# Weight pairs of the heads scaled on GpSimd, with the half-width low parts made there

## The chip, the cores and the metric

One core of one Trainium2 chip runs the whole program. Its engines are TensorE (PE: products and transposes, with the weight load PEld), VectorE (DVE), ScalarE (ACT) and GpSimd (POOL); each works through its own instructions in order and waits where one of them needs what another engine has not finished. The on-chip memory is SBUF, the product banks are PSUM, and SyncE (SP) issues DMA transfers from and to HBM. The metric is the device time of one execution in microseconds (us), as the median of several.

## The reference, cut to what matters

The layer normalises 2048 tokens of width 1024 (and 256 context tokens), multiplies them by one matrix `w_in` of 9216 columns, and splits the columns between a gated recurrence with eight heads of width 128 (five column blocks a head: query, value, two forget gates, output gate) and a short convolution (four times 1024 columns). Both meet in an output projection:

```python
h = rmsnorm(x, norm_w[l]) * (1.0 + scale[:, None]) + shift[:, None]
hc = rmsnorm(xc, norm_w[l]) * (1.0 + scale_c) + shift_c
p = h @ w_in[l]
pc = hc @ (w_in[l, :, :HG_COLS] if last else w_in[l])
...
o, _, _ = bidir_scan(q, kf, kb, v, gf, gb, s_f, s_b)
y_hg = hgrn_out(o, p[..., 4 * HG_WIDTH:HG_COLS], hg_onorm_w[l], x.dtype)
y_cv = conv_branch(p[..., HG_COLS:], conv_w[l], grid=True)
y = jnp.concatenate([y_hg, y_cv], axis=-1) @ w_out[l]
x = x + gate[:, None] * y
return rmsnorm(x, final_norm_w)
```

What this case turns on is the product `h @ w_in`, in float32.

## The kernel before

**Products in float16 parts.** A float32 operand is scaled by a power of two and kept as a float16 high part and a float16 low part (the rest); a product is then three float16 products (high by high, high by low, low by high: lines 930 to 932). `split` (L155 to L158) makes both parts of a piece of a weight block: ACT writes the high part with the scale as a factor, and DVE's SCALAR_TENSOR_TENSOR multiplies the piece by the scale again and subtracts the high part.

**Seven products for eight.** Columns are taken in pairs of blocks of 128. With the pair as a 2x2 arrangement of half-width operands, `seven` (from L917) forms the four results from seven products, in the order A11, S1, S2, A12, S3, S4, A22. Its banks are `sa`, `sb`, `sc`; `keep` (L937) is ACT's copy of a bank out of PSUM (`p1`, `p5`, `u2`), which the product that goes on in the same bank waits for, and `plus` (L941) is DVE's sum of a bank and such a copy, into `f`, `vT`, `q` or `z`. A unit is one such set of seven products for 512 tokens.

**Preparing a pair.** `load_pair` loads two blocks of the weights, 128x1024 float32 each, into `stage` (in the profile `ws_p`; `ws_p281` is block 1 of pair p28, `ws_p280` its block 0). The steps in `w.pre` have ACT sum the absolute values (L409); the nine steps in `w.rest` are: `begin` (the scale `sc_p` by three small DVE instructions at L151 to L153, and the sum S1, `s1_p`, at L424), `whole` (A11 and A12 at once: high part `whia`, low part `wloa`, 128x1024; then block 1's left half becomes A11 minus A21, L435), S1 (`whib`, `wlob`), `sum_a` (S2, over block 0's left half, L441), A22, S2, `sum_b` (S4, over block 0's right half, L444), S3, S4. The last three land in `e_p`. S1, A22, S2, S3 and S4 are 128x512 each. A pair has 128x1024 and five times 128x512 to split. The sums and differences are made of the unscaled blocks, and the scale comes in at each `split`. The first pair of each kind gets A21 too, in a place of its own (`a21_at`), for products that aren't in the scheme of seven.

There are 36 pairs: eight z pairs (the two forget gates of a head, p24 to p31), eight v pairs (value and query, p8 to p15), four gate pairs (p32 to p38, for two heads each), and sixteen of the convolution. `split_steps` hands out the steps of the next pair while a unit's products run, one each few ticks of PE: in the heads `w.gap` is 6 ticks and `w.room` 4.

**What runs beside it.** The loop goes over 8 heads by 4 segments of 512 tokens; units of the next segment run while the scan of the segment before is computed, from `chain`. A scan has seven levels. `update` (L485 on `K`, L492 on `Q`, L498 on `tot`, all DVE) works them out; ACT makes the copy `km` (L601), POOL the copy `qm` (L608, three in a segment), and PE multiplies them (L631, L650, L657) into `A`, from which DVE takes `Ac` (L639). At the end of the levels ACT copies `A` (L661) and POOL writes four diagonal pieces of `Ac` over it (L665). So before the change POOL has two kinds of work in a segment, three `qm` and four `A`.

**What sets the order.** The program is written step by step, then a scheduler of the language lays each engine's instructions in order by when it reckons them ready; the order on an engine is fixed from then on. So a step that waits longer can be put behind another.

Of the kernel before, what the change touches and what calls it, by code (L numbers as in the profile page):

```python
# [14 lines left out]
AF = mybir.ActivationFunctionType  # L15
ALU = mybir.AluOpType
# [3 lines left out]
P = 128  # L20
# [13 lines left out]
HEADS = 8  # L34
# [26 lines left out]
def hybrid_layer(ctx: ExitStack, tc, x, cx, w_ada, b_ada, w_in, w_out, fnorm_w, small_d, masks, ident_d, sel_d, out):  # L61
    nc = tc.nc
    V, S, G, PE, SY = nc.vector, nc.scalar, nc.gpsimd, nc.tensor, nc.sync
# [76 lines left out]
    def pow2_scale(rs, nm, keep=False, room=0, rb=None):  # L140
        ps = px_t(f"ss_{nm}")
        if rb is None:
            rb = sp.tile([P, 1], BF16, tag="rb", name=f"rb_{nm}", bufs=4)
            V.tensor_copy(rb, rs)
        PE.matmul(ps[:, :1], sub(rb, 0, [[0, P]]), rb, start=True, stop=True)
        if keep:
            st = cp.tile([P, 4], F32, name=f"sc_{nm}")
        else:
            st = sp.tile([P, 4], F32, tag="scale", name=f"sc_{nm}", bufs=12)
        sti = st.bitcast(I32)  # L150
        V.tensor_scalar(sti[:, 2:3], ps[:, :1].bitcast(I32), 24, None, ALU.logical_shift_right)  # L151
        V.tensor_scalar(sti[:, 0:1], sti[:, 2:3], -EXP_UNIT, (204.0 - room) * EXP_UNIT, ALU.mult, ALU.add)
        V.tensor_scalar(sti[:, 1:2], sti[:, 2:3], EXP_UNIT, (50.0 + room) * EXP_UNIT, ALU.mult, ALU.add)  # L153
        return st

    def split(st, src, hi, lo):
        S.activation(hi, src, AF.Copy, scale=st[:, 0:1])  # L157
        V.scalar_tensor_tensor(lo, src, st[:, 0:1], hi, ALU.mult, ALU.subtract)  # L158
# [80 lines left out]
    lows, casts = {}, {}  # L239
# [151 lines left out]
    def behind(fn):  # L391

        follow(last_keep, fn)

    def load_pair(col0, col1, nm, own=False, a21_at=None):

        w = W()
        stage, rs = [], []
        for i, c0 in enumerate((col0, col1)):
            sg_ = wp.tile([P, KT, P], F32, tag="stage", name=f"ws_{nm}{i}", bufs=4)  # L400
            SY.dma_start(sg_, w_in[c0 // P])
            stage.append(sg_)
        a11, a12 = stage[0][:, :HK], stage[0][:, HK:]
        a21, a22 = stage[1][:, :HK], stage[1][:, HK:]
        t = {}

        def sizes(i):
            r = sp.tile([P, 1], F32, tag="rowsum", name=f"rsum_{nm}{i}", bufs=4)
            S.activation(junk.rearrange("p (k n) -> p k n", k=KT), stage[i], AF.Abs, accum_out=r)  # L409
            rs.append(r)  # L410
            if i:
                rs.append(sp.tile([P, 1], BF16, tag="rb", name=f"rb_{nm}", bufs=4))
                S.activation(rs[2], rs[1], AF.Identity, bias=rs[0])

        def begin():
            w.st = pow2_scale(None, nm, rb=rs[2])
            pool, x = (qp, "g") if own else (wp, "w")
            nb = 1 if own else 2
            t["a"] = [pool.tile([P, KT, P], F16, tag=f"{x}{y}", name=f"w{y}a_{nm}", bufs=2 * nb) for y in ("hi", "lo")]
            t["b"] = [pool.tile([P, KT, P], F16, tag=f"{x}{y}", name=f"w{y}b_{nm}", bufs=2 * nb) for y in ("hi", "lo")]  # L420
            ee = pool.tile([P, 2, 3 * HK, P], F16, tag="ge" if own else "e", name=f"e_{nm}", bufs=nb)
            t["e"] = [ee[:, 0], ee[:, 1]]
            t["s1"] = rp.tile([P, HK, P], F32, tag="ring", name=f"s1_{nm}")
            V.tensor_tensor(t["s1"], a21, a22, ALU.add)  # L424
            w.ops = {}
            for i, (key, o) in {"A11": ("a", 0), "A12": ("a", HK), "A22": ("b", 0), "S1": ("b", HK), "S2": ("e", 0),
                                "S3": ("e", HK), "S4": ("e", 2 * HK)}.items():
                w.ops[i] = [x_[:, o:o + HK] for x_ in t[key]]
            if a21_at is not None:
                w.ops["A21"] = a21_at  # L430
                split(w.st, a21, *a21_at)

        def whole():
            split(w.st, stage[0], t["a"][0], t["a"][1])
            V.tensor_tensor(a21, a11, a21, ALU.subtract)  # L435

        def part(name, src):
            return lambda: split(w.st, src(), *w.ops[name])

        def sum_a():  # L440
            V.tensor_tensor(a11, t["s1"], a11, ALU.subtract)  # L441

        def sum_b():
            V.tensor_tensor(a12, a12, a11, ALU.subtract)  # L444

        w.pre = [lambda: behind(lambda: sizes(0)), lambda: behind(lambda: sizes(1))]
        w.rest = [begin, whole, part("S1", lambda: t["s1"]), sum_a, part("A22", lambda: a22),
                  part("S2", lambda: a11), sum_b, part("S3", lambda: a21), part("S4", lambda: a12)]
        block = col0 // P - 5 * HEADS
        w.gap, w.room = (6, 4) if block < 0 else (2, {0: 3, 1: 2}.get(block % 8, 1))  # L450
        return w

# [871 lines left out]
    def load(own):  # L1324
        wk = todo[own].pop(0)
        ws[wk] = load_pair(wk[0], wk[1], f"p{wk[0] // P}", own, extra_a21[own].pop(0) if extra_a21[own] else None)
        loaded.append(ws[wk])
        return ws[wk]
# [356 lines left out]
```

## Time and profile before

| | us |
|---|---|
| median of 3 runs | 2149.01 |
| lowest, highest | 2147.64, 2150.84 |
| profiled execution, span of core 0 | 2150.1 |
| PE busy | 2073.2 |
| DVE busy | 1645.8 |
| ACT busy | 1192.2 |
| POOL busy | 191.8 |

The profile gives a span and no time around it, so the span is what stands beside the runs. A row with a time ahead is an instruction: its start in us from the start of the span, its length in us, the engine, the line of the kernel, the operation, what it writes and reads with the numbers of the buffers left out, the size, and in brackets how long the engine stood idle before it and what ended that. A row that begins with a line number is a group of such instructions, with their number, busy us and mean ns, then the idle time before them.

```profile
PE   5988999999999999999999999999999999999998
PEld 2877878888888888888888887444444444444443
DVE  6787988878778787788687887678778656687775
ACT  7965666757567666576676654354445423333332
POOL 0121111111111110111110100000000000000000
```

These are the engines' busy shares in 40 slices of the span, in tenths. The norms and the conditioning come first, then the heads (to about 1270 us), the convolution and at the end the output projection. POOL has a tenth or two to do in the heads and next to nothing behind them.

### The profile page before, as it was taken

The page shows a single profiled execution, that of the slowest core. Times are in us where ns is not written, and L with a number is a line of the kernel's source. Part 1 is how long each engine was busy: PE and PEld are TensorE (multiplying, and loading weights), DVE is VectorE, ACT ScalarE, POOL GpSimd, SP SyncE. Part 2 cuts the span into 40 slices and gives each one's busy share as a digit, 9 for nine tenths or more (in the row PEclk, how much of TensorE's full clock was granted, in tenths as well). Part 3 has the DMA queues.
Part 4 walks back from the last instruction along what each step waited for, and adds up shares of the span by engine and source line. Part 5 has one row for each costly group of instructions (what it writes and reads, how often), then busy time and mean ns, then how long its engine had stood idle before and what let it go on. Part 6 is the DMA issues. An engine that isn't in the chain of part 4 may idle for free.

```text
span 2150.1 us, 53050 instructions
## 1 busy us (share of the span) xinstructions
PE 2073.2 (96%) x22111; PEld 1466.0 (68%) x22111; DVE 1645.8 (77%) x3413; ACT 1192.2 (55%) x2406; POOL 191.8 (9%) x272
## 2 busy tenths in 40 slices
PE   5988999999999999999999999999999999999998
PEld 2877878888888888888888887444444444444443
DVE  6787988878778787788687887678778656687775
ACT  7965666757567666576676654354445423333332
POOL 0121111111111110111110100000000000000000
PEclk9999999999999999999999999999999999999999
DMA  9567533442344233424543458933442105642421
GB/s 356 191 207 265 178 126 134 137 158 72 114 129 146 97 114 109 153 81 142 194 131 127 130 165 260 285 108 110 134 149 93 54 23 196 206 143 92 137 79 59
DMA packets 185798, 311.02 MB, mean 145 GB/s; under 512 B 13010, under 2 KB 114770, under 8 KB 183764
## 3 DMA queue, kind: packets, MB, share of 16 engines
q1 hardware_dynamic: 183396, 303.68, 42.9%
q8 instruction: 173, 2.83, 0.5%
q10 hardware_dynamic: 2160, 3.93, 0.5%
q14 instruction: 69, 0.57, 0.1%
HBM read 240.19 MB, written 67.37 MB: 143 GB/s over the span
## 4 chain that ended last, share of the span: by engine, by line
PE 65%; DVE 18%; ACT 7%; DMA 4%; issue 3%; POOL 1%; SPq 0%; POOLq 0%; ACTq 0%; DVEq 0%
PE sa L930 8%; PE sa L932 8%; PE sa L931 8%; PE sb L930 4%; PE sb L932 4%; PE sb L931 4%; PE sa_o L930 2%; PE sa_o L931 2%; PE sa_o L932 2%; DVE Q L492 2%; PE sc L930 2%; PE sc L931 2%; PE sc L932 2%; DVE K L485 2%; PE T L681 2%
## 5 line engine op out<-in xcount | busy, mean ns | idle before, releaser
L931 PEld LDWEIGHTS <-e_p 128*128 128x128 f16 x1332 | 130.4, 98 | 59.8 <-issue 10.3
L930 PEld LDWEIGHTS <-e_p 128*128 128x128 f16 x1332 | 130.4, 98 | 54.0 <-issue 1.1
L601 ACT ACTIVATE km<-K 128x512 f32<-128x512 f32 x192 | 129.6, 675 | 67.2 <-DVE K L485 61.1
L932 PEld LDWEIGHTS <-e_p 128*128 128x128 f16 x1332 | 130.3, 98 | 51.4
L485 DVE TENSOR_TENSOR K<-K,tot 128x512 f32<-128x512 f32 x192 | 132.2, 689 | 42.9 <-ACT km L601 25.3
L492 DVE TENSOR_TENSOR Q<-Q,tot 128x512 f32<-128x512 f32 x192 | 132.5, 690 | 34.9 <-POOL qm L608 19.5
L608 POOL COPY qm<-Q 128x512 f32<-128x512 f32 x96 | 80.8, 842 | 794.4 <-DVE Q L492 778.7
L931 PEld LDWEIGHTS <-whib_p 128*128 128x128 f16 x888 | 86.9, 98 | 42.1 <-issue 8.8
L930 PEld LDWEIGHTS <-whib_p 128*128 128x128 f16 x888 | 86.8, 98 | 36.7 <-issue 0.8
L930 PEld LDWEIGHTS <-whia_p 128*128 128x128 f16 x888 | 87.0, 98 | 35.7 <-DMA hop3B<-Hd3B 2.3
L932 PEld LDWEIGHTS <-wloa_p 128*128 128x128 f16 x888 | 87.0, 98 | 34.2
L931 PEld LDWEIGHTS <-whia_p 128*128 128x128 f16 x888 | 87.0, 98 | 33.9 <-issue 1.5
L932 PEld LDWEIGHTS <-wlob_p 128*128 128x128 f16 x888 | 86.8, 98 | 34.0
L157 ACT ACTIVATE e_p<-ws_p,sc_p 128x512 f16<-128x512 f32 x108 | 77.5, 718 | 54.9 <-DVE ws_p L444 42.0
L665 POOL COPY A<-Ac 32x128 f32<-32x128 f32 x128 | 77.2, 603 | 128.3 <-ACT A L661 110.6
L853 ACT ACTIVATE cv<-c,small 128x512 f32<-128x512 f32 (+1 forms) x36 | 24.2, 673 | 106.8 <-DVE c L871 61.1
L937 ACT ACTIVATE u<-sa,sx_w 128x256 f32<-128x256 f32 (+1 forms) x111 | 58.1, 524 | 43.5 <-PE sa L932 34.7
L937 ACT ACTIVATE p<-sa,sx_w 128x256 f32<-128x256 f32 (+1 forms) x111 | 57.4, 517 | 39.9 <-PE sa L932 39.8
L158 DVE SCALAR_TENSOR_TENSOR e_p<-ws_p,sc_p,e_p 128x512 f16<-128x512 f32 x108 | 79.4, 750 | 0.0
L409 ACT ACTIVATE junk<-ws_p 128x1024 f16<-128x1024 f32 x72 | 75.7, 1052 | 6.5 <-DMA ws_p<-in_w_in 6.3
L1596 POOL TENSOR_TENSOR x_o<-x_o,fw 128x512 f32<-128x512 f32 x1 | 1.3, 1262 | 868.0 <-ACT junk L1587 868.0
L937 ACT ACTIVATE p<-sb,sx_w 128x256 f32<-128x256 f32 (+1 forms) x111 | 57.8, 521 | 30.8 <-PE sb L932 28.0
(858 smaller groups left out, 7036.3 us busy)
## 6 DMA issues: line engine op xcount, KB each, us to landing
ws_p<-in_w_in SPq DMA_DIRECT2D x72, 512.0 KB, 4.3
y_o<-yT SPq DMA_DIRECT2D x32, 512.0 KB, 4.3
xt_x<-in_x SPq DMA_DIRECT2D x16, 512.0 KB, 6.2
wa<-in_w_ada SPq DMA_DIRECT2D x16, 512.0 KB, 10.2
Gd<-zs SPq DMA_DIRECT2D x32, 256.0 KB, 2.7
sg<-Gd SPq DMA_DIRECT2D x32, 256.0 KB, 4.4
wos<-in_w_out SPq DMA_DIRECT2D x32, 256.0 KB, 5.0
yT<-y SPq DMA_DIRECT2D x32, 256.0 KB, 2.9
```

The source lines that it names most:

```text
L157: S.activation(hi, src, AF.Copy, scale=st[:, 0:1])
L158: V.scalar_tensor_tensor(lo, src, st[:, 0:1], hi, ALU.mult, ALU.subtract)
L409: S.activation(junk.rearrange("p (k n) -> p k n", k=KT), stage[i], AF.Abs, accum_out=r)
L485: V.tensor_tensor(m, m, sub(cur, nb + 1, [[2, np_], [-(nb + 1), 2], [0, B]]), ALU.mult)
L492: V.tensor_tensor(m, m, sub(cur, 1, [[2, np_], [nb - 1, 2], [0, B]]), ALU.mult)
L601: S.activation(sub(s.km, 0, [[2 * B, n // (2 * B)], [B, 2], [1, B]]), mix(s.K, n, B, n // (2 * B)), AF.Copy)
L608: G.tensor_copy(sub(qm, 0, [[2 * B, n // (2 * B)], [B, 2], [1, B]]), mix(s.qf, n, B, n // (2 * B)))
L665: G.tensor_copy(A3[js, :, js], s.Ac[js])
L930: PE.matmul(ps, hi[:, k], rh, start=start and k == 0, stop=False, skip_group_check=not start)
L931: PE.matmul(ps, hi[:, k], right(name, 1, k), start=False, stop=False, skip_group_check=not start)
L932: PE.matmul(ps, lo[:, k], rh, start=False, stop=k == nk - 1, skip_group_check=not start)
L937: last_keep.append(S.activation(r, ps, AF.Copy, scale=sx))
```

## The change

For a pair of the heads that has no place for A21 (`scaled`), POOL multiplies both staged blocks by the scale in place, ahead of the first sum. Everything behind that works on scaled values: ACT copies the high parts without a factor, the five half-width low parts are a subtraction on POOL, and the low part of A11 and A12 together a subtraction on DVE. The other pairs (the first z, v and gate pair, and the convolution's) go through `split` as before. Multiplying by a power of two is exact, so what is computed stays the same.

```diff
         t = {}
+        block = col0 // P - 5 * HEADS
+        scaled = block < 0 and a21_at is None
...
             t["s1"] = rp.tile([P, HK, P], F32, tag="ring", name=f"s1_{nm}")
+            if scaled:
+                for i in (1, 0):
+                    G.tensor_scalar(stage[i], stage[i], w.st[:, 0:1], 0.0, ALU.mult, ALU.add)
             V.tensor_tensor(t["s1"], a21, a22, ALU.add)
...
+        def lows(src, hi, lo, eng):
+            if not scaled:
+                return split(w.st, src, hi, lo)
+            S.activation(hi, src, AF.Copy)
+            eng.tensor_tensor(lo, src, hi, ALU.subtract)
+
         def whole():
-            split(w.st, stage[0], t["a"][0], t["a"][1])
+            lows(stage[0], *t["a"], V)
             V.tensor_tensor(a21, a11, a21, ALU.subtract)

         def part(name, src):
-            return lambda: split(w.st, src(), *w.ops[name])
+            return lambda: lows(src(), *w.ops[name], G)
```

The lines move by some: S1's sum from L424 to L429, the difference from L435 to L446, `sum_a` from L441 to L452, `sum_b` from L444 to L455, and all behind them by 10 (`Q` from L492 to L502, `keep` from L937 to L947). The scalings are L428, the copies to the high parts L441, the low parts L442.

Three places show what the order becomes. All are around z pair p28, which is prepared for head 4 while segment 1 of head 3 is scanned (`Q_3_1`, `K_3_1`, `A_3_1`); its scale is `sc_p28`. First DVE, before:

```order
L492 TENSOR_TENSOR Q_3_1_9844<-Q_3_1_9844,tot_3_1_9867 128x32x2x8
L424 TENSOR_TENSOR s1_p28_10104<-ws_p281_8003 128x512
L485 TENSOR_TENSOR K_3_1_9341<-K_3_1_9341,tot_3_1_9867 128x16x2x16
L435 TENSOR_TENSOR ws_p281_8003<-ws_p280_8001,ws_p281_8003 128x512
L151 TENSOR_SCALAR sc_p28_10095<-ss_p28_10093 128x1
L152 TENSOR_SCALAR sc_p28_10095<-sc_p28_10095 128x1
L153 TENSOR_SCALAR sc_p28_10095<-sc_p28_10095 128x1
...
L492 TENSOR_TENSOR Q_3_1_9844<-Q_3_1_9844,tot_3_1_9867 128x16x2x16
...
L485 TENSOR_TENSOR K_3_1_9341<-K_3_1_9341,tot_3_1_9867 128x8x2x32
...
L492 TENSOR_TENSOR Q_3_1_9844<-Q_3_1_9844,tot_3_1_9867 128x8x2x32
L158 SCALAR_TENSOR_TENSOR wloa_p28_10100<-ws_p280_8001,sc_p28_10095,whia_p28_10099 128x1024
L158 SCALAR_TENSOR_TENSOR wlob_p28_10102<-s1_p28_10104,sc_p28_10095,whib_p28_10101 128x512
```

And the same place on DVE now:

```order
L502 TENSOR_TENSOR Q_3_1_9858<-Q_3_1_9858,tot_3_1_9881 128x32x2x8
L495 TENSOR_TENSOR K_3_1_9355<-K_3_1_9355,tot_3_1_9881 128x16x2x16
L151 TENSOR_SCALAR sc_p28_10109<-ss_p28_10107 128x1
...
L502 TENSOR_TENSOR Q_3_1_9858<-Q_3_1_9858,tot_3_1_9881 128x16x2x16
L429 TENSOR_TENSOR s1_p28_10118<-ws_p281_8015 128x512
L649 COPY_PREDICATED Ac_3_1_9937<-mask_127,A4_3_1_10122 128x128
L446 TENSOR_TENSOR ws_p281_8015<-ws_p280_8013,ws_p281_8015 128x512
L649 COPY_PREDICATED Ac_3_1_9937<-mask_127,A4_3_1_10122 128x128
L495 TENSOR_TENSOR K_3_1_9355<-K_3_1_9355,tot_3_1_9881 128x8x2x32
L442 TENSOR_TENSOR wloa_p28_10114<-ws_p280_8013,whia_p28_10113 128x1024
L502 TENSOR_TENSOR Q_3_1_9858<-Q_3_1_9858,tot_3_1_9881 128x8x2x32
```

The scale stands ahead of the sum (L429) and the difference (L446), which stood ahead of it; both now wait for POOL, and so do the `K` and `Q` of level 5 that stand behind them on DVE. `wloa` has moved ahead of that `Q`.

Second ACT, beside it, before (`p5_55` and `u2_55` are `keep`'s copies for a unit's products that are running, `km5_3_1` and `km0_3_0` copies for the scan):

```order
L937 ACTIVATE p5_55_10146<-sb_55_10076,sx_w47_8422 128x256
L157 ACTIVATE whia_p28_10099<-ws_p280_8001,sc_p28_10095 128x1024
L937 ACTIVATE u2_55_10169<-sa_55_10038,sx_w47_8422 128x256
L157 ACTIVATE whib_p28_10101<-s1_p28_10104,sc_p28_10095 128x512
L157 ACTIVATE whib_p28_10101<-ws_p281_8003,sc_p28_10095 128x512
L157 ACTIVATE e_p28_10103<-ws_p281_8003,sc_p28_10095 128x512
L601 ACTIVATE km0_3_0_10514<-K_3_0_9815 128x512
```

And now:

```order
L947 ACTIVATE p5_55_10162<-sb_55_10090,sx_w47_8436 128x256
L611 ACTIVATE km0_3_0_10532<-K_3_0_9829 128x512
L441 ACTIVATE whia_p28_10113<-ws_p280_8013 128x1024
L947 ACTIVATE u2_55_10185<-sa_55_10052,sx_w47_8436 128x256
L441 ACTIVATE whib_p28_10115<-s1_p28_10118 128x512
L441 ACTIVATE whib_p28_10115<-ws_p281_8015 128x512
L441 ACTIVATE e_p28_10117<-ws_p281_8015 128x512
```

`km0` has moved ahead of `whia`, and `whia`, which now waits for POOL's second scaling, still stands right ahead of `u2`.

Third POOL. Before, this stretch holds the scan's copies alone:

```order
L608 COPY qm1_3_1_9954<-Q_3_1_9844 128x512
L608 COPY qm3_3_1_10057<-Q_3_1_9844 128x512
L608 COPY qm5_3_1_10186<-Q_3_1_9844 128x512
L665 COPY A_3_1_10245<-Ac_3_1_9923 32x4x32 x4
L608 COPY qm1_3_0_10604<-Q_3_0_10294 128x512
```

And now, with p12, the v pair of head 4, behind p28 (its low parts left out here):

```order
L618 COPY qm3_3_1_10071<-Q_3_1_9858 128x512
L428 TENSOR_SCALAR ws_p281_8015<-ws_p281_8015,sc_p28_10109 128x1024
L428 TENSOR_SCALAR ws_p280_8013<-ws_p280_8013,sc_p28_10109 128x1024
L618 COPY qm5_3_1_10202<-Q_3_1_9858 128x512
L442 TENSOR_TENSOR wlob_p28_10116<-s1_p28_10118,whib_p28_10115 128x512
L442 TENSOR_TENSOR wlob_p28_10116<-ws_p281_8015,whib_p28_10115 128x512
L442 TENSOR_TENSOR e_p28_10117<-ws_p281_8015,e_p28_10117 128x512
L442 TENSOR_TENSOR e_p28_10117<-ws_p280_8013,e_p28_10117 128x512
L675 COPY A_3_1_10261<-Ac_3_1_9937 32x4x32 x4
L442 TENSOR_TENSOR e_p28_10117<-ws_p280_8013,e_p28_10117 128x512
L428 TENSOR_SCALAR ws_p121_10105<-ws_p121_10105,sc_p12_10437 128x1024
L428 TENSOR_SCALAR ws_p120_10103<-ws_p120_10103,sc_p12_10437 128x1024
```

`qm5` stands behind both scalings of p28, the four `A` copies behind four of its low parts, and the `qm1` of the next segment behind everything of p12.

More of the change, by code (lines that the diff above doesn't have):

```diff
@@ L448, in load_pair @@
                   part("S2", lambda: a11), sum_b, part("S3", lambda: a21), part("S4", lambda: a12)]
-        block = col0 // P - 5 * HEADS
         w.gap, w.room = (6, 4) if block < 0 else (2, {0: 3, 1: 2}.get(block % 8, 1))
```

## The prediction

> **What bounds the kernel now.** I read the page's busy times first, then busy times by stretch, then the waits of TensorE (PE), and last the timeline around one weight pair.
>
> ```profile
> span 2150.1 us, 53050 instructions
> ...
> PE 2073.2 (96%) x22111; PEld 1466.0 (68%) x22111; DVE 1645.8 (77%) x3413; ACT 1192.2 (55%) x2406; POOL 191.8 (9%) x272
> ...
> 470.00:610.00 140.00, 138.24 (x2137) 122.63 (x2139) 109.23 (x240) 86.42 (x197) 18.18 (x24) 1.00 0.35 111
> 610.00:760.00 150.00, 147.35 (x2241) 130.35 (x2230) 121.59 (x272) 99.81 (x221) 21.92 (x32) 1.00 0.38 125
> ```
>
> The first two lines are the page's: PE is busy for 96% of the span. The other two are stretches inside the heads; after start, end and length their columns are PE, its weight loads, VectorE (DVE), ScalarE (ACT), GpSimd (POOL), then the granted clock, which is full. In the first stretch PE is busy for 138.24 of 140 us, DVE for 109.23 (78%), ACT for 86.42 (62%), POOL for 18.18 (13%). So work taken from DVE is not taken from the time: at most PE's 1.8 us of idle time in such a stretch can be won, and whatever makes PE wait longer is paid in full.
>
> PE's waits in the heads (190 to 1270 us), the largest; each row names the product that waits, what it waits for, and us in total, times, the longest:
>
> ```profile
> PE A L631 <- POOL qm L608: 7.6, 10, 2.7
> PE sa L930 <- ACT u L937: 3.3, 11, 0.6
> PE sa L930 <- DVE f L941: 3.1, 7, 1.2
> PE A L650 <- POOL qm L608: 2.7, 2, 1.5
> PE A L631 <- DVE Q L492: 2.1, 8, 0.3
> PE T L681 <- ACT kT L674: 1.6, 3, 0.8
> PE sa L930 <- ACT p L937: 1.6, 2, 1.1
> PE sb L930 <- DVE f L941: 1.3, 1, 1.3
> ```
>
> They come to 23.3 us. Many are short, which says that ACT's and DVE's evacuations of the product banks (`u`, `p`, `f`) arrive close to the moment PE needs them. That closeness decides this case.
>
> **The change part by part.** It touches 17 weight pairs: seven z pairs, seven v pairs, three gate pairs (eight, eight and four there are; the first of each kind has a place for A21 and stays as it was). For each:
>
> *DVE loses work.* The five half-width low parts leave it:
>
> ```profile
> L158 DVE SCALAR_TENSOR_TENSOR e_p<-ws_p,sc_p,e_p 128x512 f16<-128x512 f32 x108 | 79.4, 750 | 0.0
> ```
>
> Five of 750 ns are 3.75 us a pair, 64 us in all. The full-width low part stays, as a subtraction without the scale; I cost that difference at nothing. ACT keeps its instructions at their sizes, only without a scale: nothing.
>
> *POOL gains work.* Two scalings of 128x1024 and five subtractions of 128x512 a pair. Nearest rows:
>
> ```profile
> 632.85 0.61 POOL L608 COPY qm<-Q 128x512 f32<-128x512 f32 x1 [3.54 <-DVE Q L492]
> ...
> 2132.68 1.26 POOL L1596 TENSOR_TENSOR x_o<-x_o,fw 128x512 f32<-128x512 f32 x1 [868.04 <-ACT junk L1587]
> ```
>
> A one-input pass over 512 columns takes 0.61 us undisturbed, so 1024 columns are put at 1.22. A two-input pass takes 1.26. That is 2x1.22 + 5x1.26 = 8.7 us a pair, 148 us in all; POOL has the room (18 of 140 us used). The bounds for one subtraction are 0.61 (as if the second input cost nothing) and 1.26 plus one wait for DVE of 0.69, so 1.95; I take 1.26, the row of the same operation.
>
> [...]
>
> *The operands themselves are not late.* The z pair that is prepared at 640 us, in front of head 4's first unit:
>
> ```profile
> 648.00 1.40 DVE L158 SCALAR_TENSOR_TENSOR e_p<-ws_p,sc_p,e_p 128x512 f16<-128x512 f32 x2
> ...
> 659.08 0.27 PE L930 MATMUL sa<-hop15B,whia_p 128*128 128x256 f16 x1
> ...
> 632.90:669.40 36.50, 35.94 (x491) 31.56 (x488) 34.52 (x73) 27.91 (x51) 5.60 (x7) 1.00 0.20 65
> ```
>
> Its last two low parts end at 649.4, and PE reads the pair first at 659.08. POOL needs 8.7 us for what DVE did in about 5, so the last low part comes some 4 to 6 us later and is still in time. What costs is who waits meanwhile, and the third row says that this is a tight place: between 632.9 and 669.4, where a z pair and a v pair are prepared beside a scan, DVE works for 34.52 of 36.5 us and PE for 35.94.
>
> *The new wait in a z pair.* Before:
>
> ```profile
> 637.43 0.14 DVE L153 TENSOR_SCALAR sc_p<-sc_p 128x1 int32<-128x1 int32 x1
> ...
> 637.83 0.69 DVE L492 TENSOR_TENSOR Q<-Q,tot 128x512 f32<-128x512 f32 x1
> ...
> 639.24 1.14 ACT L157 ACTIVATE whia_p<-ws_p,sc_p 128x1024 f16<-128x1024 f32 x1
> 640.27 0.46 ACT L937 ACTIVATE u<-sa,sx_w 128x256 f32<-128x256 f32 x1
> ...
> 640.79 0.27 PE L930 MATMUL sa<-hop15T,e_p 128*128 128x256 f16 x1 [0.27 <-ACT u L937]
> ...
> 642.98 0.63 PE L657 MATMUL A<-Q,K 128*32 128x64 f32 x32
> ```
>
> The scale is ready at 637.57. Behind it POOL now runs two scalings, to 640.0, or to 640.7 if DVE's `Q` (0.69) gets between them. `whia` on ACT waits for the second: it ends at 641.2 to 641.9, and `u`, which stands right behind it on ACT, at 641.6 to 642.3. Before, `u` ended at 640.73 and PE, already waiting, went on at 640.79. So PE stands 0.9 to 1.6 us longer. DVE's queue gives about the same: the sum and the difference wait for the scalings, then come `K`, `wloa`, and `Q` of level 5, which also needs POOL's copy `qm` that is queued behind the scalings; `Q` ends near 643.9 to 644.6, against PE's need at 642.98 plus the stall. The four `A` copies of the level results, which PE's next products need, now stand on POOL between low parts. Lower end: nothing, if the scheduler's new place of `whia` happened to be covered by another wait of PE; the rows show none there. Upper end: 1.6 us, as worked out. I take the upper end, **1.6 us**, because the five POOL subtractions that follow contend with DVE as well.
>
> *The new wait in a v pair.* Before:
>
> ```profile
> 659.00 0.15 DVE L153 TENSOR_SCALAR sc_p<-sc_p 128x1 int32<-128x1 int32 x1
> ...
> 659.12 1.15 ACT L157 ACTIVATE whia_p<-ws_p,sc_p 128x1024 f16<-128x1024 f32 x1 [2.71 <-DVE sc_p L152]
> 660.17 0.58 ACT L740 ACTIVATE Q<-o 128x512 f32<-128x512 f32 x1
> ...
> 666.98 0.49 ACT L937 ACTIVATE u<-sa,sx_w 128x256 f32<-128x256 f32 x1
> ...
> 667.51 0.27 PE L930 MATMUL sa<-hop15T,e_p 128*128 128x256 f16 x1
> ```
>
> The scale comes earlier, near 657.8, since the sum and the difference (about 0.69 each) now stand behind it; two scalings end at 660.3 to 661.0, so `whia` begins 1.2 to 1.9 us later. Copy `Q` (0.58) goes ahead of it and gives 0.5 back. ACT then works without a gap up to `u` (ends 667.47), for which PE's product at 667.51 waits: 0.7 to 1.4 us, less about 0.2 that PE waits nearby already, so 0.5 to 1.2. I take the middle, **0.9 us**.
>
> *A gate pair.* Here `whia` and two `whib` stand before the two evacuations `kT`:
>
> ```profile
> 686.74 1.15 ACT L157 ACTIVATE whia_p<-ws_p,sc_p 128x1024 f16<-128x1024 f32 x1 [1.72 <-DVE sc_p L152]
> 687.80 0.71 ACT L157 ACTIVATE whib_p<-s_p,sc_p 128x512 f16<-128x512 f32 x1
> 688.41 0.71 ACT L157 ACTIVATE whib_p<-ws_p,sc_p 128x512 f16<-128x512 f32 x1
> 689.02 1.06 ACT L674 ACTIVATE kT<-kT 128x512 f32<-128x512 f32 x2
> ```
>
> `whia` moves from 686.74 to about 688.4 (two scalings after a scale that comes 0.7 earlier, since the sum stands behind it now), but both `whib` (0.61 apart) go behind `kT`: `kT` lands 0.4 to 1.0 later. PE waits for it already (the row `PE T <- ACT kT` above, 1.6 us over three times, the longest 0.8), so nothing hides that. I take the middle again, **0.7 us**.
>
> *Sum.* 7x1.6 + 7x0.9 + 3x0.7 = 11.2 + 6.3 + 2.1 = 19.6 us on the span of 2150.1, so 2169.7. The median of the runs, 2149.0, is 1.1 below that span (the page shows nothing around the span): **2168.6**.
>
> **The rivals.**
>
> *Faster: relief without a handoff price.* DVE has 64 us less to do, 6.5 of PE's 23.3 us of waits name DVE itself (`f` and `Q` in the rows above: 3.1, 2.1, 1.3), more hang on it through `qm`, and over the stretch DVE is busy 78% and ACT 62% of the time, so a late `whia` might be absorbed. If a third of the 23.3 us went and nothing were added, the time is 2149.0 less 7.8, 2141. For it: DVE has no free time at the tight place, and 3.75 us a pair is what it lacks. Against it: at the points above PE has 0.06 us to spare.
>
> *No change.* The delays and the relief meet: 2149, give or take 4.
>
> *Slower by more: the port.* POOL and DVE hold each other up:
>
> ```profile
> 632.87 0.75 DVE L833 SCALAR_TENSOR_TENSOR y<-oT,small,sg 128x512 f32<-128x512 f32 x1
> ...
> 638.65 1.14 POOL L608 COPY qm<-Q 128x512 f32<-128x512 f32 x1 [5.19 <-DVE Q L492]
> ...
> 638.64 0.69 DVE L485 TENSOR_TENSOR K<-K,tot 128x512 f32<-128x512 f32 x1
> ...
> 41.53 4.13 DVE L312 TENSOR_TENSOR hop<-h_x,hop 128x512 f16<-128x512 f32 x4
> ...
> 41.30 1.80 POOL L301 TENSOR_SCALAR hop<-h_x 128x512 f16<-128x512 f32 x2
> ```
>
> A copy on POOL takes 0.61 us (the row at 632.85 above) beside `y`, one of whose inputs is in PSUM, but 1.14 beside `K`, both of whose inputs are in SBUF: it gets through when `K` is done. In the other direction DVE's two-input instructions take 1.03 us each (4.13 by four) beside POOL's, where `K` takes 0.69. If the two take turns throughout, a pair adds 8.7 us of POOL's turns and frees 3.75: 5.0 us more on what is full between 632.9 and 669.4. If half of that reaches PE, 17x2.5 = 42 us on 2149: **2191**. It decides once DVE's slack at the evacuations, 0.06 us to about 2, is used up. I hold it less likely than the forecast because `f`, `vT`, `z` and the like, which come from PSUM, run beside POOL as `y` did, and because late low parts have 9 us to spare. [...]
>
> *The change doesn't do what it says.* The rows of the order in the section on the change show the scalings and the low parts on POOL, so this is given no chance.
>
> **How the numbers follow.** Forecast (2157 to 2180): 0.50. Port (2180 to 2200): 0.15. No change: 0.15. Faster: 0.20. The range reaches from 2142 (half of the faster case left out) to 2186 (part of the port left out). About 0.2% is what a measurement can tell from no change, 4.3 us: faster 0.20, same 0.15, slower 0.65.
>
> **What would show it.** In the profile after: POOL near 340 us; DVE some 60 us less; ACT `whia` idle before it, named POOL; PE's waits on ACT `u` risen from 3.3 to over 10 us; DVE waiting for `ws_p` from POOL at the sum; scalings near 1.2 us, subtractions 1.3 to 2. If `whia` starts no later than before, or PE's waits stay near 23 us, the steps on the waits are wrong; if POOL's instructions take twice their undisturbed time and DVE's busy time does not fall, the port rival holds.

## The result and the profile after

The changed kernel takes 2249.62 us (median of 5 runs, 2241.57 to 2253.35), the kernel before 2150.79 us (5 runs). The ratio is 1.0457, 95% interval 1.0438 to 1.0475: 98.8 us between the medians and 98 by the ratio, where 19.6 had been forecast. The profiled execution's span rose from 2150.1 to 2247.8 us, by 97.7. The five executions go with the clock that TensorE was granted: 0.985 on average in the two shortest, 0.978 to 0.980 in the three others. The page's busy times, of the changed kernel:

```profile
span 2247.8 us, 53160 instructions
...
PE 2100.1 (93%) x22111; PEld 1483.3 (66%) x22111; DVE 1678.0 (75%) x3328; ACT 1185.4 (53%) x2406; POOL 367.2 (16%) x391
```

Two things stand out. DVE issues 85 instructions fewer, which had taken 64 us, and yet it is busy 32 us longer (1645.8 before). And PE, with the same 22111 instructions, is busy 26.9 us longer (2073.2 before). PE's waits in the heads, which now last longer (190 to 1370 us; 190 to 1270 in the prediction's list), in us in total, times, the longest:

```profile
PE sa L940 <- ACT u L947: 27.2, 14, 3.5
PE oT L841 <- ACT kT L684: 15.0, 5, 3.0
PE A L641 <- POOL qm L618: 12.1, 12, 2.1
PE vt_c L565 <- ACT vT_c L560: 10.1, 3, 3.4
PE A L667 <- DVE Q L502: 7.2, 6, 3.4
PE A L641 <- DVE Q L502: 6.0, 12, 1.2
PE sb L940 <- DVE vT L951: 4.9, 6, 1.3
```

`u`, put at over 10 us by the prediction, has 27.2 (3.3 before). But `oT`, `vt_c`, the level-5 `Q` (L667) and `vT`, which stood nowhere in the list before, come to another 37 us. No row names a low part made by POOL: the operands are in time, as forecast. Summed over all its gaps between 190 and 1400 us, PE stands 100.2 us, 30.9 before. So the 97.7 us of span are 69.3 us of standing, 26.9 us in which PE is busy longer with the same products (its clock, by the last section), and 1.5 us elsewhere.

What DVE and POOL spent, by groups of instructions (count, busy us, mean ns). First DVE before, then DVE and POOL of the changed kernel:

```profile
L492 DVE TENSOR_TENSOR Q<-Q,tot 128x512 f32<-128x512 f32 x192 | 132.5, 690 | 34.9 <-POOL qm L608 19.5 <-PE A L631 15.3
L485 DVE TENSOR_TENSOR K<-K,tot 128x512 f32<-128x512 f32 x192 | 132.2, 689 | 42.9 <-ACT km L601 25.3 <-PE A L657 17.5
...
L485 DVE TENSOR_TENSOR K<-K,f 128x512 f32<-128x512 f32 x32 | 35.7, 1117 | 0.5
...
L441 DVE TENSOR_TENSOR ws_p<-s_p,ws_p 128x512 f32<-128x512 f32 x36 | 24.6, 684 | 0.0
```

```profile
L502 DVE TENSOR_TENSOR Q<-Q,tot 128x512 f32<-128x512 f32 x192 | 151.9, 791 | 35.0 <-POOL qm L618 18.1 <-PE A L641 16.8
L495 DVE TENSOR_TENSOR K<-K,tot 128x512 f32<-128x512 f32 x192 | 137.4, 716 | 45.6 <-ACT km L611 26.5 <-PE A L667 18.9
L495 DVE TENSOR_TENSOR K<-K,f 128x512 f32<-128x512 f32 x32 | 43.0, 1342 | 0.5
...
L452 DVE TENSOR_TENSOR ws_p<-s_p,ws_p 128x512 f32<-128x512 f32 x36 | 35.0, 972 | 0.1
...
L442 POOL TENSOR_TENSOR e_p<-ws_p,e_p 128x512 f16<-128x512 f32 x51 | 79.8, 1577 | 2.9 <-ACT e_p L441 2.0
...
L428 POOL TENSOR_SCALAR ws_p<-ws_p,sc_p 128x1024 f32<-128x1024 f32 x34 | 51.5, 1526 | 114.8 <-issue 54.4 <-DVE sc_p L153 43.2 <-ACT Q L750 11.8
```

`Q` went from 690 to 791 ns, `K` from 689 to 716, the first `K` of a scan (`K<-K,f`) from 1117 to 1342, and `sum_a` from 684 to 972. All of them have two inputs in SBUF, the change did not alter their sizes or engine, and all of them are longer now. POOL's subtraction takes 1577 ns on average, where 1.26 us had been taken from a row in which POOL was alone.

Where it hurts is seen around the z pair that the prediction followed (p28, now prepared from 677 us on). DVE and POOL, in order of time:

```profile
682.36 1.21 DVE L442 TENSOR_TENSOR wloa_p<-ws_p,whia_p 128x1024 f16<-128x1024 f32 x1
683.50 1.64 DVE L502 TENSOR_TENSOR Q<-Q,tot 128x512 f32<-128x512 f32 x1
685.06 0.47 DVE L951 SCALAR_TENSOR_TENSOR vT<-sc,sx_w,p 128x256 f32<-128x256 f32 x1
685.46 1.25 DVE L452 TENSOR_TENSOR ws_p<-s_p,ws_p 128x512 f32<-128x512 f32 x1
...
687.03 1.25 DVE L495 TENSOR_TENSOR K<-K,tot 128x512 f32<-128x512 f32 x1
688.20 1.64 DVE L502 TENSOR_TENSOR Q<-Q,tot 128x512 f32<-128x512 f32 x1
...
692.17 2.08 DVE L495 TENSOR_TENSOR K<-K,f 128x512 f32<-128x512 f32 x1
...
682.59 2.00 POOL L442 TENSOR_TENSOR wlob_p<-s_p,whib_p 128x512 f16<-128x512 f32 x1 [1.50 <-ACT whib_p L441]
684.56 1.60 POOL L442 TENSOR_TENSOR wlob_p<-ws_p,whib_p 128x512 f16<-128x512 f32 x1
...
691.78 1.47 POOL L442 TENSOR_TENSOR e_p<-ws_p,e_p 128x512 f16<-128x512 f32 x1
```

POOL's first subtraction begins while `wloa` runs and is stretched to 2.00 us; DVE's `Q`, which follows, takes 1.64 us for 0.69. `vT`, which reads PSUM, keeps its 0.47 (0.48 before). The ends show how: POOL's subtraction ends at 684.59, `Q` 0.55 us later at 685.14, POOL's second 1.02 after that at 686.16, `sum_a` 0.55 after that at 686.71. The two engines finish in turn, and each stretched instruction lasts until the other engine's is done and then most of its own time (0.55 of 0.69, 1.02 of 1.26 us): in these rows they take turns by whole instructions. At 692.17 `K` takes 2.08 us for 1.1, beside the subtraction that began at 691.78. The five stretched DVE rows (1.64, 1.25, 1.25, 1.64 and 2.08 us) are together 4.0 us longer than their kind before. ACT and PE behind it:

```profile
680.57 1.06 ACT L441 ACTIVATE whia_p<-ws_p 128x1024 f16<-128x1024 f32 x1 [0.76 <-POOL ws_p L428]
681.53 0.46 ACT L947 ACTIVATE u<-sa,sx_w 128x256 f32<-128x256 f32 x1
...
694.28 0.70 ACT L611 ACTIVATE km<-K 128x512 f32<-128x512 f32 x1 [2.04 <-DVE K L495]
694.87 1.09 ACT L684 ACTIVATE kT<-kT 128x512 f32<-128x512 f32 x2
...
682.04 0.27 PE L940 MATMUL sa<-hop15T,e_p 128*128 128x256 f16 x1 [1.79 <-ACT u L947]
...
695.52 0.69 PE L841 MATMUL oT<-ident,Q 128*128 128x128 f32 x2 [3.00 <-ACT kT L684]
```

The first stop is the one forecast: `whia` waits for POOL, `u` stands behind it, PE stands 1.79 us (0.27 before, 1.6 forecast on top). The second, 3.00 us, names ACT's `kT`, but ACT was idle for 2.04 us: `kT` is queued behind `km`, and `km` waits for the `K` that took 2.08 us and began late, at the end of these stretched rows on DVE.

### The profile page after: what moved, and what is told of

Same layout as the page of the kernel before. It is cut to its first block, busy times and chain, and to the rows that moved or that the text cites. A ratio compares the mean times of both kernels' runs of the same rounds, so it can differ in the third digit from the quotient of the medians.

```text
span 2247.8 us, 53160 instructions
## 1 busy us (share of the span) xinstructions
PE 2100.1 (93%) x22111; PEld 1483.3 (66%) x22111; DVE 1678.0 (75%) x3328; ACT 1185.4 (53%) x2406; POOL 367.2 (16%) x391
## 4 chain that ended last, share of the span: by engine, by line
PE 65%; DVE 19%; ACT 5%; issue 4%; DMA 4%; POOL 3%; SPq 0%; POOLq 0%; ACTq 0%; DVEq 0%
PE sa L940 8%; PE sa L942 8%; PE sa L941 8%; PE sb L940 4%; PE sb L942 4%; PE sb L941 4%; DVE Q L502 3%; DVE K L495 3%; PE sa_o L940 2%; PE sa_o L941 2%; PE sa_o L942 2%; PE sc L940 2%; POOL ws_p L428 2%; PE sc L942 2%; PE sc L941 2%
## 5 line engine op out<-in xcount | busy, mean ns | idle before, releaser
L941 PEld LDWEIGHTS <-e_p 128*128 128x128 f16 x1332 | 132.6, 100 | 85.0 <-issue 33.4
L502 DVE TENSOR_TENSOR Q<-Q,tot 128x512 f32<-128x512 f32 x192 | 151.9, 791 | 35.0 <-POOL qm L618 18.1
L495 DVE TENSOR_TENSOR K<-K,tot 128x512 f32<-128x512 f32 x192 | 137.4, 716 | 45.6 <-ACT km L611 26.5
L940 PEld LDWEIGHTS <-e_p 128*128 128x128 f16 x1332 | 132.6, 100 | 56.0 <-issue 1.1
L942 PEld LDWEIGHTS <-e_p 128*128 128x128 f16 x1332 | 132.7, 100 | 53.5
L947 ACT ACTIVATE u<-sa,sx_w 128x256 f32<-128x256 f32 (+1 forms) x111 | 58.1, 523 | 58.9 <-PE sa L942 49.6
L675 POOL COPY A<-Ac 32x128 f32<-32x128 f32 x128 | 71.4, 557 | 101.8 <-ACT A L671 94.5
L442 POOL TENSOR_TENSOR e_p<-ws_p,e_p 128x512 f16<-128x512 f32 x51 | 79.8, 1577 | 2.9 <-ACT e_p L441 2.0
L947 ACT ACTIVATE p<-sa,sx_w 128x256 f32<-128x256 f32 (+1 forms) x111 | 57.5, 518 | 36.8 <-PE sa L942 36.5
L947 ACT ACTIVATE p<-sb,sx_w 128x256 f32<-128x256 f32 (+1 forms) x111 | 57.8, 521 | 33.2 <-PE sb L942 30.3
L157 ACT ACTIVATE hiS_o<-y_o,sc_y 128x1024 f16<-128x1024 f32 x32 | 36.8, 1148 | 69.0 <-PE sa_o L941 31.3
```

The lines of the kernel that those rows point to most:

```text
L442: eng.tensor_tensor(lo, src, hi, ALU.subtract)
L495: V.tensor_tensor(m, m, sub(cur, nb + 1, [[2, np_], [-(nb + 1), 2], [0, B]]), ALU.mult)
L502: V.tensor_tensor(m, m, sub(cur, 1, [[2, np_], [nb - 1, 2], [0, B]]), ALU.mult)
L675: G.tensor_copy(A3[js, :, js], s.Ac[js])
L940: PE.matmul(ps, hi[:, k], rh, start=start and k == 0, stop=False, skip_group_check=not start)
L941: PE.matmul(ps, hi[:, k], right(name, 1, k), start=False, stop=False, skip_group_check=not start)
```

## The experiments

Each run is compared with the kernel before, measured beside it on the same chip (2148.9 to 2149.9 us). "The 98 us" are the changed kernel's loss.

### The scalings alone

```diff
-            return lambda: lows(src(), *w.ops[name], G)
+            return lambda: lows(src(), *w.ops[name], V)
```

> GpSimd keeps the two scalings of each of the 17 pairs; the five half-width low parts are subtractions on DVE. Theory port (the five subtractions on GpSimd and DVE's two-input instructions hold each other up, and that is most of the loss of 98 us): most of it comes back; what remains is the wait for the scalings, PE's waits for ACT u of some 25 us, and a little clock: 2170 to 2190 us. Theory handoff (the wait of whia, of the sum and of the difference for GpSimd's scalings is most of the loss): still above 2225 us.

Measured: 2181.77 us, ratio 1.0151 (1.0136 to 1.0166), 33 us of the 98. Its waits and busy times:

```profile
PE 2076.2 (95%) x22111; PEld 1468.3 (67%) x22111; DVE 1655.8 (76%) x3413; ACT 1185.0 (54%) x2406; POOL 241.1 (11%) x306
...
PE sa L940 <- ACT u L947: 23.2, 18, 2.3
...
L502 DVE TENSOR_TENSOR Q<-Q,tot 128x512 f32<-128x512 f32 x192 | 133.1, 693 | 31.4 <-POOL qm L618 15.8 <-PE A L641 15.5
```

`Q` is back at 693 ns, and PE's waits for `u` are still there. So the loss has two parts, and the subtractions are the larger one: with them on POOL as well it is 65 us more. PE's waits for `u` rise by 19.9 us, near the 19.6 that the prediction had put the whole handoff at. Luck has a part in that: its terms for `u` were 17.5 of the 19.6, six z pairs stop for `u` by 1.8 to 2.3 us as forecast (0.27 before, 1.6 on top), the v pairs by 1.15 to 1.8 where 0.9 was forecast, and the waits for `kT` of the gate pairs rise by 1.5 us (3.1 after 1.6) and not by 2.1.

### The subtractions alone, the scalings on DVE

```diff
-                    G.tensor_scalar(stage[i], stage[i], w.st[:, 0:1], 0.0, ALU.mult, ALU.add)
+                    V.tensor_scalar(stage[i], stage[i], w.st[:, 0:1], 0.0, ALU.mult, ALU.add)
```

> DVE makes the two scalings, GpSimd the five half-width low parts. Theory port: the loss stays for the most part, since the subtractions are still on GpSimd, and DVE has two instructions more a pair: 2210 to 2240 us. Theory handoff: with no scaling on GpSimd to wait for, near the kernel before: 2149 to 2170 us.

Measured: 2219.47 us, ratio 1.0341 (1.0307 to 1.0374), 70.5 us. With the scalings on POOL alone 33 us, with the subtractions on POOL alone 70.5: together 103, the changed kernel 98. That is near, but this run also gives DVE 34 scalings of 0.76 us, 26 us (POOL's take 1.53 each), so the 70.5 are not the subtractions' alone.

### Subtractions on POOL that nobody waits for

```diff
+                if block < 0 and a21_at is None:
+                    d = sp.tile([P, HK, P], F16, tag="dum", name=f"d_{nm}{name}", bufs=1)
+                    G.tensor_tensor(d, sub(ident, 0, [[0, HK], [1, P]]), hi, ALU.subtract)
```

This stands in the kernel before, behind each half-width `split` of the 17 pairs; the low parts stay on DVE, and nothing reads `d`.

> The kernel before with all its low parts on DVE, and beside each of the 85 half-width ones a subtraction of the same size on GpSimd that reads the high part and a constant, and whose result nobody reads. Theory port: DVE's K and Q instructions are stretched as in the changed kernel, to 0.75 us and above on average, while DVE keeps its 64 us of low parts: 2220 to 2260 us. Theory handoff: nobody waits for these subtractions but the scan's copies queued behind them on GpSimd: 2149 to 2160 us.

Measured: 2230.95 us, ratio 1.0376 (1.036 to 1.0391), 82 us. No product waits for anything new, no operand moved, and POOL's results are thrown away. The time is in the port theory's range, with `K` and `Q` a little under its 0.75 us (724 and 729 ns). What is left as the cause is POOL at work beside DVE: something that the two share, or POOL's own fuller queue. The next run tells these apart.

### POOL just as busy, but only writing

```diff
-                    G.tensor_tensor(d, sub(ident, 0, [[0, HK], [1, P]]), hi, ALU.subtract)
+                    G.tensor_tensor(d[:, 0, :4], ident[:, :4], hi[:, 0, :4], ALU.subtract)
+                    for _ in range(3):
+                        G.memset(d, 0.0)
```

> As the one before, but GpSimd fills the dummy (one tiny subtraction of 4 columns and three memsets, which only write) in place of each subtraction. Theory port, in the form that the shared reading of SBUF is what holds DVE up: DVE's K and Q stay at 0.69 us and the time near the kernel before, 2149 to 2165 us. Theory of a busy queue (what hurts is that the scan's qm and A copies stand behind other work on GpSimd): as slow as the run with subtractions, above 2200 us, as far as the fills take as long.

Measured: 2165.72 us, ratio 1.008 (1.0065 to 1.0095), 17 us, 0.7 us above what the port theory allowed. The two runs beside each other, with reads and with fills; each time the page's busy times, then DVE's `Q` and low parts:

```profile
PE 2094.4 (94%) x22111; PEld 1478.6 (66%) x22111; DVE 1719.8 (77%) x3413; ACT 1194.3 (54%) x2406; POOL 307.3 (14%) x357
...
L498 DVE TENSOR_TENSOR Q<-Q,tot 128x512 f32<-128x512 f32 x192 | 139.9, 729 | 35.3 <-POOL qm L614 17.9 <-PE A L637 17.4
...
L158 DVE SCALAR_TENSOR_TENSOR e_p<-ws_p,sc_p,e_p 128x512 f16<-128x512 f32 x108 | 94.2, 887 | 0.0
```

```profile
PE 2075.8 (96%) x22111; PEld 1468.0 (68%) x22111; DVE 1647.5 (76%) x3413; ACT 1193.8 (55%) x2406; POOL 365.5 (17%) x612
...
L500 DVE TENSOR_TENSOR Q<-Q,tot 128x512 f32<-128x512 f32 x192 | 132.3, 689 | 48.5 <-POOL qm L616 33.1 <-PE A L639 15.4
```

With fills POOL is busy for 365.5 us, as in the changed kernel and 58 us more than with reads, and DVE is within 2 us of its old 1645.8 us, with `Q` at its old 689 ns. With reads DVE is busy 74 us longer than before. So it is the sharing that costs, and in these two runs only with an instruction that reads. The fills' 17 us go with queueing: DVE's `Q` is idle 33.1 us behind POOL's `qm` copies, 19.5 before. What the two engines share, no trace names; what the runs show is lengths: `Q` and the low parts, both with two inputs in SBUF, take 729 and 887 ns on average with reads, and with fills 689 and 750, as before.

### The scalings without PE's evacuation behind them

In the kernel with the scalings alone, three empty steps are put between the scalings and the first sum, and `whia` is held behind ACT's latest `keep` (`first` is the sum S1):

```diff
+        w.rest = [begin] + [lambda: None] * (3 if scaled else 0) + [first, whole, part("S1", lambda: t["s1"]), sum_a,
...
-            lows(stage[0], *t["a"], V)
+            (behind if scaled else lambda f: f())(lambda: lows(stage[0], *t["a"], V))
```

> Low parts on DVE and scalings on GpSimd as in the run with the scalings alone (2181.8 us), but three empty steps stand between the scalings and the first sum, and the copy whia is held behind ACT's latest copy of a product bank, so that u2 no longer stands behind it on ACT. Theory order (the scalings cost because u, for which PE waits, is queued behind the waiting whia, and DVE's K and Q behind the waiting sum): PE's waits for ACT u fall from 23 to about 4 us, and the time to 2149 to 2160 us. Theory room (it is GpSimd's 50 us of scalings themselves, their reads of SBUF and the qm copies behind them): still 2170 us or more.

Measured: 2163.81 us, ratio 1.0069 (1.0052 to 1.0085): 14 us in place of 33, between the two theories. Its waits:

```profile
PE sa L942 <- ACT u L949: 11.3, 10, 1.9
...
PE oT L843 <- ACT kT L686: 6.6, 5, 1.3
```

At the z pairs the stop for `u` is gone (around p28 `u` ends at 645.80, and PE goes on at 645.85), but five of them stop for 1.3 us at `oT` instead, where `kT` stands behind a high-part copy that waits for `sum_a` on DVE. Three v pairs still stop for `u` by 1.3 to 1.7 us, and the three gate pairs, which had no such stop, by 1.4 to 1.9. The order explains over half of the scalings' cost. Part of the rest may be sharing, since POOL's 51.6 us of scalings read SBUF too and `K` is at 723 ns (689 with the scalings alone); that was not separated.

### The same order with the subtractions on POOL

As the run before, with `part` on POOL again.

> The same change of places, with the five low parts on GpSimd as in the changed kernel (2249.6 us). If the two losses add up, this takes off what the wait for the scalings costs alone (33 us) and leaves the subtractions' part: 2210 to 2225 us. If they share the time (DVE, already late by the subtractions, hides the wait), it takes off less: 2230 us or more.

Measured: 2205.32 us, ratio 1.027 (1.0248 to 1.0291), 55 us, 44 us less than the changed kernel and a little below the range. The losses do not share the time, but they do not simply add up either: the same change of places took 19 us off the scalings alone and takes 44 off here, more than the 33 that the scalings cost. In the old order the wait and the stretching make each other dearer; through which wait was not tried. This order alone does not rescue the change.

### One kind of pair at a time

```diff
-        scaled = block < 0 and a21_at is None
+        scaled = block < 0 and a21_at is None and col0 // HG == ZB_
```

> The change for the seven z pairs alone. In the changed kernel PE stands about 1.8, 0.8, 0.7 and 3.0 us at each of them, 6.3 us by seven, 44 us, and about half of the 27 us of slower clock follows those stops: 2195 to 2215 us. If the port costs the same at each pair, 7/17 of 98 us: 2190 us, the same within reach; if the pairs only cost together (DVE's lateness carried from one to the next), below 2175 us.

Measured: 2192.88 us, ratio 1.0199 (1.0184 to 1.0215), 43 us or 6.1 a pair. With `V_` in its place, the v pairs alone:

> The change for the seven v pairs alone. In the changed kernel PE stands about 2 us at each of them and 2.9 us more behind three of them: 23 us. Theory that each pair pays for itself: 2170 to 2175 us with the clock at full speed, up to 2183 us if two or three of the stops fall so that a window at half clock follows. Theory that pairs cost only through DVE's lateness carried over from the z pair before: below 2160 us.

Measured: 2180.46 us, ratio 1.0149 (1.0135 to 1.0163), 30.6 us or 4.4 a pair. With `GATE_`, the gate pairs alone:

> The change for the three gate pairs alone. PE's stops there in the changed kernel are 1.0 and 3.4 us at each, 13 us in all: 2162 us with the clock at full speed, up to 2172 us with a window or two at half clock behind each of the longer stops. Carried-over lateness alone: below 2155 us.

Measured: 2166.67 us, ratio 1.009 (1.0074 to 1.0105), 17 us or 5.6 a pair. The three come to 90 us of the 98, so nearly all of it is paid pair by pair. The forecast's 1.6, 0.9 and 0.7 us are short in every kind by 3.5 to 5 us; the dummy subtractions, at 82 us, cost 4.8 us a pair.

### Taking POOL out of the scan in the kernel before

Had the sharing cost the kernel before something too? `qm` made by DVE:

```diff
-            G.tensor_copy(sub(qm, 0, [[2 * B, n // (2 * B)], [B, 2], [1, B]]), mix(s.qf, n, B, n // (2 * B)))
+            V.tensor_copy(sub(qm, 0, [[2 * B, n // (2 * B)], [B, 2], [1, B]]), mix(s.qf, n, B, n // (2 * B)))
```

> The kernel before, with the scan's three qm copies a segment made by DVE ahead of its update of Q and not by GpSimd. If sharing with GpSimd and the handoff to it cost more than DVE's own copy, PE's 10 us of waits named qm go and the time falls to 2135 to 2147 us; if DVE's 96 copies of some 0.4 to 0.7 us come on top of where it is full, 2150 to 2175 us.

Measured: 2147.6 us, ratio 0.9989 (0.998 to 0.9999), 2 us less, between the two ranges and too little to count on.

```profile
L608 DVE COPY qm<-Q 128x512 f32<-128x512 f32 x90 | 37.9, 421 | 0.0
...
PE A L631 <- DVE Q L492: 5.7, 9, 1.3
PE A L631 <- DVE qm L608: 3.9, 5, 1.7
```

A copy takes DVE 0.42 us instead of POOL's 0.84, and PE's waits for `qm` fall from 10.3 us to 5.6 (3.9, and 1.7 in the other product), but its waits for `Q` rise from 2.1 to 5.7. With the four pieces of `A` on ACT as well:

```diff
-                G.tensor_copy(A3[js, :, js], s.Ac[js])
+                S.activation(A3[js, :, js], s.Ac[js], AF.Copy)
```

> The kernel before with GpSimd taken out of the scan altogether: DVE makes the qm copies, as in the run that gave 2147.6 us, and ACT the four pieces of A. If what GpSimd still costs the scan is its sharing and its handoffs, a little less again: 2138 to 2146 us; if ACT's 128 small copies (some 0.2 to 0.3 us each, some 30 us in all) delay its evacuations, 2150 to 2165 us.

Measured: 2153.47 us, ratio 1.0016 (1.0007 to 1.0024). The 128 copies take ACT 39 us, and PE's waits for ACT's `u` rise to 6.7 us (3.3 before). No version here beats the kernel before by more than about a tenth of a per cent.

## Why the prediction was wrong, point by point

- **What bounds the kernel** held: PE waits, and what it waits for is paid in full. That its clock would stay full did not hold; see below.
- **The operands are in time** held: no wait of PE names a low part.
- **The new waits behind the scalings** held as a mechanism, at the place named. Their size was short: the scalings alone cost 33 us, of which the rise of PE's waits for `u` is 19.9; that this is so near the sum of 19.6 is in part luck, since the single terms miss in both directions.
- **POOL's subtractions cost nothing but their time on POOL** is the step that failed. The sum has no term for them; that they "contend with DVE as well" served only to choose 1.6 us, the upper end of a wait for the scalings. Durations were taken from rows in which each engine was alone (1.26 us, 0.69 us), and DVE was counted 64 us lighter. It is 32 us busier instead: 96 us of stretching on what was left to it by its busy time, 77 by the summed lengths of its instructions. By the difference to the run with the scalings alone, the subtractions on POOL make 65 of the 98 us. The dummy subtractions show the cost without any of the change's waits: 82 us, there with DVE's own low parts still on DVE.
- **The port as a rival** was therefore the main term, and was handled wrongly in two ways. It got a chance of 0.15, although its own rows spoke for it (the 1.14 us copy beside `K`, the 1.03 us instructions beside POOL's); the reasons held against it, that PSUM readers go undisturbed (`vT` takes 479 ns on average before and after) and low parts have time to spare (no wait of PE names one), are both true here and beside the point, since `K` and `Q` of the scan, which PE needs at once, are the two-input instructions. And it was priced on 2149, as if it took the place of the handoff; the runs show that both are paid. 19.6 + 42 would have been 2211, still 39 us short. Of its two signs one came (DVE's busy time did not fall) and the other did not: POOL's instructions took 1.25 to 1.36 times the forecast's, not twice.
- **The clock** was not in the sum at all: PE is busy 26.9 us longer with the same products. This is no third cause beside the scalings and the subtractions but comes behind the stops that they make: 3.0 us with the scalings alone, 22.3 with the subtractions alone (PE busy 2076.2 and 2095.5 us).
- **Relief of DVE** as a reason for faster never came about; 64 us were freed and 77 to 96 taken.

## What to carry to other kernels

Before work is moved from VectorE to GpSimd, list what VectorE runs beside it. Here that had two inputs in SBUF and sat on the critical path, and GpSimd's subtractions, which read SBUF, were paid for on VectorE, whoever waited for their results (82 us for 85 results that nobody read, with `Q` at 729 ns for 690). Do not price a rival as an alternative when nothing stops it from happening in addition. A control that keeps an engine at least as busy with instructions that only write (three fills for a subtraction) separated sharing from queueing here in one run (POOL busy for 365.5 us, DVE's `Q` at 689 ns).

## What was not expected of the hardware

**TensorE's granted clock halved in stretches of 3.413 us that lie on one grid.** In the heads the granted clock of the changed kernel is at 0.50 only in stretches of 3.413 us or twice that, and all of them begin on one grid of 3.413 us. Around the 3.00 us stop at `oT`, in windows of that grid (start and end, length, then busy us of PE, its weight loads, DVE, ACT, POOL, and the granted clock), first of the changed kernel, then of the run with z pairs alone, which stops there for 3.00 us too (to 672.63):

```profile
691.25:694.67 3.42, 1.27 (x12) 0.98 (x10) 3.42 (x5) 1.38 (x4) 1.93 (x2) 1.00 0.12 24
694.67:698.08 3.41, 2.56 (x12) 2.06 (x13) 3.34 (x8) 2.39 (x5) 0.00 (x0) 0.50 0.35 130
698.08:701.50 3.42, 3.42 (x18) 3.12 (x16) 1.27 (x5) 2.02 (x4) 0.00 (x0) 0.50 0.20 77
701.50:704.91 3.41, 3.41 (x33) 3.12 (x32) 1.53 (x4) 1.42 (x4) 0.00 (x0) 1.00 0.00 0
```

```profile
667.45:670.87 3.42, 2.17 (x19) 1.79 (x18) 3.42 (x4) 1.36 (x3) 2.78 (x3) 1.00 0.06 25
670.87:674.28 3.41, 1.65 (x15) 1.53 (x16) 3.34 (x8) 2.60 (x5) 0.00 (x0) 1.00 0.46 154
674.28:677.69 3.41, 3.41 (x33) 3.24 (x32) 3.13 (x9) 2.99 (x7) 0.00 (x0) 1.00 0.20 77
```

In the first, PE stands for 2.15 us of one window, and two windows at half clock follow: 18 instructions in a full window where there are 33 at full clock (the same products `T<-v,kT` follow each other every 0.21 us up to 701.5 and every 0.11 us from there). In the second the same stop is cut by the grid into 1.25 and 1.76 us, and nothing happens. In the heads of the changed kernel the clock fell behind 16 windows at full clock, in which PE stood for 2.05 to 3.02 us, and behind none in which it stood for 1.86 us or less; in the kernel before it fell behind one of 2.66 us, and behind none of 1.48 us or less. So PE need not stand throughout a window: 2.05 of 3.41 us were enough. The changed kernel has 20 windows at half clock in the heads, the kernel before one, the z pairs alone two although they stop for 3.0 us at five heads. So a part of the 98 us, up to the 26.9, hangs on where the stops fall on the grid; that was read from the traces and not tried by moving the stops.
